# SSM layer: the next group's four x tiles ahead of z and their turn behind it, an output half and the later group's B and C after that, the decay exponents behind the third x

## The chip, the cores and the metric

The kernel runs on one core of one Trainium2 chip. The metric is device microseconds of one execution, as the median of several runs. TensorE (PE in the profile) multiplies matrices into PSUM, which has eight banks; VectorE (DVE) and ScalarE (ACT) read PSUM and work element by element; GpSimd (POOL) does elementwise work in SBUF alone; SyncE (SP) issues most transfers. Each engine takes its instructions in order and waits on semaphores for the others.

## The reference

One inference step of a two-layer hybrid model on 256 prompt tokens and 8 x 16 sample tokens, 384 tokens in all. Layer 0 has a short convolution and an attention, layer 1 is a state space mixer (SSM), and each layer ends in a feed-forward block with a convolution. The change touches only the SSM mixer:

```python
def odd_mixer(h, conv_state, ssm_state, w_in, conv_w, conv_b, dt_bias, a_log, d_skip, norm_w, w_out):
    proj = h @ w_in
    z, xbc, dt_raw = jnp.split(proj, [D_INNER, D_INNER + CONV_DIM], axis=-1)
    xbc, new_conv = causal_dwconv(xbc, conv_state, conv_w, conv_b)
    xbc = jax.nn.silu(xbc)
    xs, bm, cm = jnp.split(xbc, [D_INNER, D_INNER + SSM_GROUPS * D_STATE], axis=-1)
    dt = jax.nn.softplus(dt_raw.astype(f32) + dt_bias.astype(f32))
    a = -jnp.exp(a_log.astype(f32))
    y, h_last = ssd_scan(xs, dt, a, bm, cm, ssm_state, chunk)
    y = y + d_skip.astype(f32)[:, None] * xs.astype(f32)
    y = y.reshape(b, length, D_INNER) * jax.nn.silu(z.astype(f32))
    y = rms_norm(y.reshape(b, length, SSM_GROUPS, D_INNER // SSM_GROUPS), norm_w).reshape(b, length, D_INNER)
    return y.astype(h.dtype) @ w_out, new_conv, h_last
```

The scan forms, in each of four groups of eight heads, a product of C and B, weights it with decays exp(cum[q] - cum[s]) and dt, multiplies it with x, adds what comes from the state, and updates the state.

## The kernel before

All products are in float32 precision, made of three passes: a weight piece is split into a high part `wh` (ScalarE, L389 and L394) and a low part `wl` (VectorE, L390 and L395), the activations likewise into `Hh` and `Hl`, and `three` (L434) adds the products high-high, high-low and low-high. Weights come in one long stream of pieces of 128 x 1024, in the order in which `_pack` writes them (L83 to L151); `Weights.take` (L398) hands them out, and there are three buffers each for the raw piece, `wh` and `wl`. A piece is split as soon as TensorE is done with the piece three before it. Pieces of the output matrix are also scaled with the norm's gain; the table `gain` (L368) names them by their place in the stream.

The SSM layer goes through four groups (L1260). Per group it needs: one tile each of B and C and four tiles of x, every one a projection block of 24 matmuls (`conv4`, L951, in the profile `xbc`), then evacuated by VectorE into `pad` in two halves, scaled by ScalarE (`c`), three taps by VectorE (`c`), and a silu by ScalarE in two parts (`B`, `C`, `xf`). `turn_bc` (L993) makes the products of C and B (`cb`, masked into `CB` by VectorE) and turns B (`bT`); `turn_x` (L1018) turns the four x tiles in 12 transposes (`xT`), which ScalarE copies into `xt`. `decays` (L1031) loads the decay rows by four transfers (`td`), subtracts and clips on ScalarE, 16 instructions, and takes four exponents. `Group.__init__` multiplies `CB` into them, and into `mix` for the sample tokens, and makes the weighted copies of x, `xdt` on VectorE and `xw` on GpSimd. `skip` loads the eight old states (`h0`) and makes the skip terms. `within` is the part inside a group (`S`, `y`), `inter` what comes from the state (`yi`), `states` four state products `hn` at a time, which VectorE adds to `h0` before ScalarE's queue stores them. `project_z` is z, four pieces and 72 matmuls of 512 columns into three banks; `Gate` multiplies silu(z) in and makes the norm, `turn` turns the result (`yT`), and `add_out` is the group's share of the output product (`op`), four quarters of one piece, 24 matmuls each.

PSUM is split in the layer into three banks for the long products (`pmm`: `xbc`, `z`, `op`) and five for the others (`paux`), and each kind goes round. A product can begin only when the bank's last reader is done. The x tiles have four buffers, so the next group's tiles can be written once the last turn is over.

From L1218 to L1319 `T.keep` holds TensorE to the order in which the program is written. All other engines' orders are made by a scheduler. The order of a group before, for TensorE: `within`, `inter(2)`, one x tile (or 48 matmuls of `op`), `inter(1)`, `turn_bc`, another x tile, `states(0)`, z, `states(1)`, two x tiles, the later group's B, `turn_x`, its C, then the next group. Ahead of group 0 stand B, C and one x tile, then the sums of decays (`E`, `cT`, `sgS`, L1224 to L1248), which need dA, the end of a long chain of small VectorE instructions (`log1pexp`, L337).

Of the kernel before, what the change touches and what calls it, by code (L numbers as in the profile page):

```python
# [14 lines left out]
ALU = mybir.AluOpType  # L15
# [67 lines left out]
def _pack(x):  # L83
# [44 lines left out]
    def out(g, cs):  # L128
        for c in cs:
            for kt in range(4 * g, 4 * g + 4):  # L130
                blocks.append(wo[kt * P:(kt + 1) * P, c:c + 256])

    bc(0, 0), bc(1, 0), xs(0), bc(0, 1), bc(1, 1)
    for g in range(4):
        if 0 < g < 3:
            out(g - 1, (0, 256))
        if g < 3:
            xs(g + 1, (0, 1))
        if g == 1:
            out(0, (512, 768))  # L140
        tm(wi, 512 * g)
        if g < 3:
            xs(g + 1, (2, 3))
        if g < 2:
            bc(0, g + 2), bc(1, g + 2)
        if g == 2:
            out(1, (512, 768))
    out(2, (0, 256, 512, 768)), out(3, (0, 256, 512, 768))
# [95 lines left out]
def build(nc, tc, d, stop=None):  # L244
# [119 lines left out]
    class Weights:  # L364
        def __init__(self):
            self.tiles, self.made, self.raw, self.pos = {}, 0, None, 0

            t = 32 + 3 * NF + 8  # L368
            self.gain = {t + i: 4 * (0 if i < 16 else 1 if i < 36 else 2 if i < 44 else 3)
                         for i in (10, 11, 14, 15, 24, 25, 34, 35, *range(40, 48))}  # L370
            self.total = d["w"].shape[0] * (RC // WC)
# [675 lines left out]
    class Group:  # L1047

        def __init__(self, g, decs, bc, xt):
            self.g, self.h8, self.xt = g, slice(8 * g, 8 * g + 8), xt  # L1050
            self.Cg, self.Cm, self.CB, self.Bt, self.Bm = bc
            self.mix, self.xdt, self.xw, self.ys = [decs[0:2], decs[2:4]], [], [], []
            for b in range(2):
                for half in self.mix[b]:
                    tt(half, half, self.CB[:, b, :].unsqueeze(1).broadcast_to([P, 4, P]), ALU.mult)
            for b in range(3):
# [7 lines left out]
            mix = t512("mix", 1, (P, 8, P))  # L1064
            dsv = decS[:, 128 * g:128 * g + 128].rearrange("p (h j) -> p h j", j=LB)
            tt(mix.rearrange("p h (b j) -> p h b j", j=LB),
               tok_s(self.CB[:, 2, :]).unsqueeze(1).broadcast_to([P, 8, NB, LB]),
               dsv.unsqueeze(2).broadcast_to([P, 8, NB, LB]), ALU.mult)
            self.mix.append([mix[:, 0:4, :], mix[:, 4:8, :]])
# [68 lines left out]
    def project_z():  # L1138
        ps = yield from tm_group("z")
        zs = t512("zs", 1, (P, 3, 512))  # L1140
        for b in range(3):
            act(zs[:, b, :], ps[b], AF.Silu, scale=r[:, b:b + 1])
        return zs
# [76 lines left out]
    xs = [conv_x(0, 0)]  # L1220
# [30 lines left out]
    xs.append(conv_x(0, 1))  # L1251
    bc_ = turn_bc(0, Bn, Cn)
    xs += [conv_x(0, 2), conv_x(0, 3)]
    Bn = conv_bc(0, 1)
    xt = turn_x(xs)
    grp = Group(0, decs, bc_, xt)
    grp.skip()
    Cn = conv_bc(1, 1)
    op = gate = None
    for g in range(4):  # L1260
# [20 lines left out]
        if g == 1:  # L1281
            steps(op)
        zs = run(project_z())
        gate = Gate(grp.ys, False)
        for b in range(3):
            gate.part(b, zs)
        gate.factor()
        grp.states(1)
        xs += [conv_x(g + 1, 2), conv_x(g + 1, 3)]
        if g < 2:  # L1290
            Bn = conv_bc(0, g + 2)
        else:
            steps(op, 8)
        xt = turn_x(xs)
        grp = Group(g + 1, decs, bc_, xt)
        if g < 2:
            Cn = conv_bc(1, g + 2)
        else:
            steps(op)
# [43 lines left out]
```

## Time and profile before

| what | value |
|---|---|
| median of 3 runs (lowest to highest) | 1098.91 us (1098.24 to 1102.22) |
| the profiled execution | 1099.84 us, of which its span 1098.0 us |
| SSM layer, from its first projection to the next layer's first matmul | 459 to 816 us |
| in it: TensorE, VectorE, ScalarE, GpSimd busy | 315, 271, 186, 105 us of 357 |
| granted TensorE clock, mean of the span | 0.981 |

The busy times of the layer are the sums of its windows. A busy share is an average over stretches with different limits: VectorE with 271 of 357 is not the bound on the whole, but it may be where its instructions stand close. In the rows of the profile, `out<-in` names what an instruction writes and reads by the program's names, then come partitions x elements; in brackets stands the idle time of the engine just before it and what ended it. All VectorE products come from one helper line (L313), all ScalarE ones from L319, all matmuls from L253, so that they are told apart by their tiles.

### The profile page before, as it was taken

What the parts mean: (1) busy time and instruction counts of PE and PEld (TensorE: products, weight loads), DVE (VectorE), ACT (ScalarE), POOL (GpSimd) and SP (SyncE); (2) the same over time, 40 slices, a digit from 0 to 9 for tenths busy, and PEclk for the clock granted to TensorE, in tenths of its full rate; (3) what the DMA queues carried; (4) which work ended last, traced back from release to release, by engine and by line L of the source; (5) the groups of instructions that cost most, each with busy time, mean ns of one, the idle gap of its engine ahead of it and who ended that gap; (6) DMA issues with size and microseconds to landing.
All of it is one profiled execution on the core that took longest, in us unless ns stands there. A gap on an engine that the chain in (4) does not pass through costs nothing.

```text
span 1098.0 us, 16780 instructions
## 1 busy us (share of the span) xinstructions
PE 1045.0 (95%) x6316; PEld 972.7 (89%) x6316; DVE 740.5 (67%) x1329; ACT 491.9 (45%) x815; POOL 151.0 (14%) x383
## 2 busy tenths in 40 slices
PE   9999999999999999967997997998999999999998
PEld 6788899999999999957686885876899999999998
DVE  6968666767767544457777958768897776775332
ACT  6344334544444333347656445552564444443221
POOL 0030000100000000013606205416001000000000
PEclk9999999999999999978998998998999999999999
DMA  8452534343434434344273553462543444344441
GB/s 270 155 167 65 167 119 133 123 130 121 134 120 131 136 122 135 115 134 128 88 267 107 156 177 129 147 197 71 173 135 122 123 127 134 120 132 131 148 149 42
DMA packets 50329, 150.31 MB, mean 137 GB/s; under 512 B 5992, under 2 KB 8312, under 8 KB 50248
## 3 DMA queue, kind: packets, MB, share of 16 engines
q1 hardware_dynamic: 44360, 136.78, 40.1%
q10 hardware_dynamic: 4608, 8.39, 2.0%
q0 software_dynamic: 1280, 4.06, 1.0%
q8 instruction: 50, 0.82, 0.3%
q14 instruction: 31, 0.25, 0.1%
HBM read 135.81 MB, written 13.40 MB: 136 GB/s over the span
## 4 chain that ended last, share of the span: by engine, by line
PE 40%; DVE 9%; ACT 3%; DMA 3%; issue 2%; SPq 0%; DVEq 0%; ACTq 0%; POOL 0%
PE fd L253 8%; PE fg L253 8%; PE fa L253 8%; PE z L253 6%; PE op L253 4%; DVE wl L313 2%; PE xbc L253 2%; DVE c L316 2%; ACT wh L319 1%; DVE wl L316 1%; PE xT L258 1%; DMA raw<-w 1%; DVE pad L313 1%; PE y L253 1%; PE hn L253 1%
## 5 line engine op out<-in xcount | busy, mean ns | idle before, releaser
L313 DVE TENSOR_TENSOR wl<-raw,wh 128x1024 fp32r<-128x1024 f32 (+1 forms) x205 | 261.1, 1274 | 152.9 <-ACT wh L319 152.5
L319 ACT ACTIVATE wh<-raw 128x1024 fp32r<-128x1024 f32 (+1 forms) x205 | 216.1, 1055 | 249.3 <-PE fd L253 95.0
L253 PE MATMUL fg<-Hh,wh 128*128 128x384 f32 x352 | 118.4, 336 | 1.0 <-DVE pad L313 1.0
L253 PE MATMUL fa<-Hl,wh 128*128 128x384 f32 x352 | 118.7, 337 | 0.3 <-DVE Hl L316 0.3
L253 PE MATMUL fg<-Hl,wh 128*128 128x384 f32 x352 | 118.6, 337 | 0.0
L253 PE MATMUL fa<-Hh,wl 128*128 128x384 f32 x352 | 118.4, 336 | 0.0
L253 PE MATMUL fg<-Hh,wl 128*128 128x384 f32 x352 | 118.4, 336 | 0.0
L253 PE MATMUL fa<-Hh,wh 128*128 128x384 f32 x352 | 118.3, 336 | 0.0
L253 PE MATMUL fd<-hh,wh 128*128 128x384 f32 x352 | 118.3, 336 | 0.0
L253 PE MATMUL fd<-hh,wl 128*128 128x384 f32 x352 | 118.3, 336 | 0.0
L253 PE MATMUL fd<-hl,wh 128*128 128x384 f32 x352 | 118.3, 336 | 0.0
L316 DVE SCALAR_TENSOR_TENSOR c<-pad,prm,c 128x400 f32<-128x400 f32 (+1 forms) x160 | 103.0, 647 | 11.7 <-ACT c L319 9.8
L253 PE MATMUL xbc<-Hh,wh 128*128 128x384 f32 x192 | 68.9, 359 | 0.7 <-DVE X L313 0.7
L253 PEld LDWEIGHTS fg<-Hh,wh 128*128 128x128 f32 x352 | 66.2, 188 | 1.3 <-ACT R L319 1.3
L253 PEld LDWEIGHTS fa<-Hl,wh 128*128 128x128 f32 x352 | 66.2, 188 | 0.8 <-DVE Hl L316 0.6
L253 PEld LDWEIGHTS fa<-Hh,wl 128*128 128x128 f32 x352 | 66.2, 188 | 0.1
L253 PEld LDWEIGHTS fg<-Hh,wl 128*128 128x128 f32 x352 | 66.2, 188 | 0.1
L253 PEld LDWEIGHTS fg<-Hl,wh 128*128 128x128 f32 x352 | 66.2, 188 | 0.1
L253 PEld LDWEIGHTS fa<-Hh,wh 128*128 128x128 f32 x352 | 66.2, 188 | 0.1
L253 PE MATMUL xbc<-Hl,wh 128*128 128x384 f32 x192 | 66.2, 345 | 0.0
L253 PE MATMUL xbc<-Hh,wl 128*128 128x384 f32 x192 | 66.2, 345 | 0.0
L253 PEld LDWEIGHTS fd<-hl,wh 128*128 128x128 f32 x352 | 66.2, 188 | 0.0
(803 smaller groups left out, 2134.1 us busy)
## 6 DMA issues: line engine op xcount, KB each, us to landing
raw<-w SPq DMA_DIRECT2D x219, 512.0 KB, 3.5
kc<-kc SPq DMA_DIRECT2D x8, 256.0 KB, 4.8
vc<-vc SPq DMA_DIRECT2D x8, 256.0 KB, 3.2
X<-x SPq DMA_DIRECT2D x8, 192.0 KB, 4.4
o_y<-X SPq DMA_DIRECT2D x8, 192.0 KB, 2.7
o_v<-vt POOLq DMA_DIRECT2D x3, 256.0 KB, 2.6
o_k<-kraw POOLq DMA_DIRECT2D x3, 256.0 KB, 3.3
cst<-cst SPq DMA_DIRECT2D x1, 617.0 KB, 6.0
```

The source lines that it names most:

```text
L253: ins = nc.tensor.matmul(*a, **kw)
L258: ins = nc.tensor.transpose(*a, **kw)
L313: (eng or V).tensor_tensor(out=out, in0=a, in1=b, op=op)
L316: V.scalar_tensor_tensor(out=out, in0=a, scalar=s, in1=b, op0=op0, op1=op1)
L319: S.activation(out, a, f, **kw)
```

## The change

The x tiles of the next group are now all projected ahead of z, and turned behind it. In group 0 three of them stand ahead of the decay sums, and the fourth, and both B and C of group 1, ahead of the turn; the four decay exponents thereby come behind the third x tile. Both calls of `states` stand ahead of z. The next group's decay products and `mix` (`Group.__init__`) stand ahead of z too; what needs the turned x is put into a new method `take`, behind it. After that come the output half (groups 1 and 2), the later group's B and C, and after group 0 one x tile of group 2. z takes two weight pieces of 512 at a time and runs both through the first two token blocks, then through the third. The weights are packed in the new order and the table of gains follows it. Nothing that is computed changes.

```diff
-    bc(0, 0), bc(1, 0), xs(0), bc(0, 1), bc(1, 1)
-    for g in range(4):
...
+    bc(0, 0), bc(1, 0), xs(0), bc(0, 1), bc(1, 1), xs(1), tm(wi, 0)
+    bc(0, 2), bc(1, 2), xs(2, (0,)), out(0, (0, 256)), xs(2, (1, 2, 3)), tm(wi, 512), out(0, (512, 768))
+    bc(0, 3), bc(1, 3), xs(3), tm(wi, 1024), out(1), tm(wi, 1536), out(2), out(3)
...
     def project_z():
-        ps = yield from tm_group("z")
+
+        ps = [pmm(f"z{b}") for b in range(3)]
+        for k0 in range(0, KT, 2):
+            ws = [W.take(512) for _ in range(2)]
+            for bs in ((0, 1), (2,)):
+                for i, (wh, wl) in enumerate(ws):
+                    for b in bs:
+                        o = slice(b * P, (b + 1) * P)
+                        three(ps[b], Hh[:, k0 + i, o], Hl[:, k0 + i, o], wh, wl, k0 + i == 0, k0 + i == KT - 1)
+                        yield
...
     Cn = conv_bc(1, 0)
-    xs = [conv_x(0, 0)]
+    xs = [conv_x(0, i) for i in range(3)]
...
     decs = decays(0)
-    xs.append(conv_x(0, 1))
-    bc_ = turn_bc(0, Bn, Cn)
-    xs += [conv_x(0, 2), conv_x(0, 3)]
-    Bn = conv_bc(0, 1)
-    xt = turn_x(xs)
-    grp = Group(0, decs, bc_, xt)
+    grp = Group(0, decs, turn_bc(0, Bn, Cn))
+    xs.append(conv_x(0, 3))
+    Bn, Cn = conv_bc(0, 1), conv_bc(1, 1)
+    grp.take(turn_x(xs))
     grp.skip()
-    Cn = conv_bc(1, 1)
+    xs = [conv_x(1, 0)]
...
         decs = decays(g + 1)
-        if g:
+        if g == 0:
+            xs.append(conv_x(1, 1))
+        elif g == 1:
             steps(op, 16)
         else:
-            xs = [conv_x(1, 0)]
+            xs = [conv_x(g + 1, 0)]
         grp.inter(1)
         bc_ = turn_bc(g + 1, Bn, Cn)
-        xs = [conv_x(g + 1, 0)] if g else [*xs, conv_x(g + 1, 1)]
+        xs.append(conv_x(g + 1, len(xs)))
         grp.states(0)
-        if g:
-            xs.append(conv_x(g + 1, 1))
-        if g == 1:
-            steps(op)
+        while len(xs) < 4:
+            xs.append(conv_x(g + 1, len(xs)))
+        grp.states(1)
+        nxt = Group(g + 1, decs, bc_)
         zs = run(project_z())
         gate = Gate(grp.ys, False)
         for b in range(3):
             gate.part(b, zs)
+        xt = turn_x(xs)
         gate.factor()
-        grp.states(1)
-        xs += [conv_x(g + 1, 2), conv_x(g + 1, 3)]
...
+        grp = nxt
+        grp.take(xt)
+        if g:
+            steps(op)
         if g < 2:
-            Cn = conv_bc(1, g + 2)
-        else:
-            steps(op)
+            Bn, Cn = conv_bc(0, g + 2), conv_bc(1, g + 2)
+        if g == 0:
+            xs = [conv_x(2, 0)]
         grp.skip()
```

TensorE's order at z of group 0, before: one state product of four, then z, whose three banks are z_5335 to z_5337, from the first matmul on.

```order
L253 MATMUL hn<-xw__5027,Bm__4851 128x512 x4
L253 MATMUL z_5335<-wh,Hh 128x512
L253 MATMUL z_5335<-wl,Hh 128x512
L253 MATMUL z_5335<-wh,Hl 128x512
L253 MATMUL z_5336<-wh,Hh 128x512
L253 MATMUL z_5336<-wl,Hh 128x512
L253 MATMUL z_5336<-wh,Hl 128x512
L253 MATMUL z_5337<-wh,Hh 128x512
```

The same place of the change, behind its second hn (one more block of 24 `xbc` matmuls stands between the first hn and this one), up to the point where the third bank, z_5455, is first written:

```order
L240 MATMUL z_5453<-wh,Hl 128x512
L240 MATMUL z_5454<-wh,Hh 128x512
L240 MATMUL z_5454<-wl,Hh 128x512
L240 MATMUL z_5454<-wh,Hl 128x512
L240 MATMUL z_5453<-wh,Hh 128x512
L240 MATMUL z_5453<-wl,Hh 128x512
L240 MATMUL z_5453<-wh,Hl 128x512
L240 MATMUL z_5454<-wh,Hh 128x512
L240 MATMUL z_5454<-wl,Hh 128x512
L240 MATMUL z_5454<-wh,Hl 128x512
L240 MATMUL z_5455<-wh,Hh 128x512
```

The first two rows of z, left out above, follow the second hn directly. The third bank is first written twelve matmuls behind the start of z instead of six, and both state products stand ahead of it.

VectorE's order at the same place, before: `h__...` are the states, to which the products hn are added, `c_5308` the taps of the last x tile ahead of z, `mix` the sample tokens' decay products of group 1, and `wl` behind them weight splits of z.

```order
L313 TENSOR_TENSOR h__5031<-h__5031,hn 128x512
L313 TENSOR_TENSOR h__5035<-h__5035,hn 128x512
L316 SCALAR_TENSOR_TENSOR c_5308<-pad_5301,prm,c_5308 128x408
L313 TENSOR_TENSOR h__5039<-h__5039,hn 128x512
L316 SCALAR_TENSOR_TENSOR c_5308<-pad_5301,prm,c_5308 128x408
L313 TENSOR_TENSOR h__5043<-h__5043,hn 128x512
L316 SCALAR_TENSOR_TENSOR c_5308<-pad_5301,prm,c_5308 128x408
L313 TENSOR_TENSOR td__5191<-td__5191,CB__5255 128x512
L313 TENSOR_TENSOR mix__5670<-CB__5255,decS 128x1024
L313 TENSOR_TENSOR wl<-raw,wh 128x1024 x3
```

And in the change, from the second of these additions on; `pad_5413` is the evacuation of the fourth x tile, whose bank is z's third:

```order
L300 TENSOR_TENSOR h__5081<-h__5081,hn 128x512
L303 SCALAR_TENSOR_TENSOR c_5354<-pad_5347,prm,c_5354 128x408
L300 TENSOR_TENSOR h__5085<-h__5085,hn 128x512
L303 SCALAR_TENSOR_TENSOR c_5354<-pad_5347,prm,c_5354 128x408
L300 TENSOR_TENSOR h__5089<-h__5089,hn 128x512
L303 SCALAR_TENSOR_TENSOR c_5354<-pad_5347,prm,c_5354 128x408
L300 TENSOR_TENSOR td__5237<-td__5237,CB__5301 128x512
L300 TENSOR_TENSOR mix__5451<-CB__5301,decS 128x1024
L300 TENSOR_TENSOR pad_5413<-xbc,R 128x256
L300 TENSOR_TENSOR wl<-raw,wh 128x1024
L300 TENSOR_TENSOR pad_5413<-xbc,R 128x8x16
L300 TENSOR_TENSOR h__5079<-h__5079,hn 128x512
```

The order up to `mix` is the same; behind it stands the new tile's evacuation in two halves around a weight split, and then the second set of additions.

ScalarE's order ahead of the turn of group 0 (`xt`), before: the last x tile is `xf__4902`, made of `c_4941`, and the table load for its silu stands ahead of the second tile's, `xf__4792`, two tiles earlier.

```order
L319 ACTIVATE xf__4856<-c_4895 128x256
L319 ACTIVATE xf__4856<-c_4895 128x128
L319 ACTIVATE c_4941<-pad_4934,prm 128x408
L319 ACTIVATE c_4987<-pad_4980,prm 128x408
L319 ACTIVATE xf__4902<-c_4941 128x256
L319 ACTIVATE xf__4902<-c_4941 128x128
```

And in the change, where only the fourth tile, `xf__4908`, stands behind the exponents of `td`:

```order
L306 ACTIVATE td__4874<-td__4874 128x512
L306 ACTIVATE Bm__4897<-bT,cst 128x128 x2
L306 ACTIVATE c_4947<-pad_4940,prm 128x408
L306 ACTIVATE c_4993<-pad_4986,prm 128x408
L306 ACTIVATE wh<-raw 128x1024
L306 ACT_TABLE_LOAD
L306 ACTIVATE xf__4908<-c_4947 128x256
L306 ACTIVATE xf__4908<-c_4947 128x128
```

Three of the four tiles' silus now stand ahead of the exponents, where only the first stood before; the two that moved stand between two table loads more than before. The fourth has stayed behind the exponents, behind a weight copy and a table load.

More of the change, by code (lines that the diff above doesn't have):

```diff
@@ L126, in xs, with out @@
         fm(wi, [2048 + 512 * g + P * i for i in tiles])
-    def out(g, cs):
+    def out(g, cs=(0, 256, 512, 768)):
         for c in cs:
@@ L131, in out @@
                 blocks.append(wo[kt * P:(kt + 1) * P, c:c + 256])
-    bc(0, 0), bc(1, 0), xs(0), bc(0, 1), bc(1, 1)
-    for g in range(4):
[L135 to L138, printed above, removed]
-        if g == 1:
[L140 to L148, printed above, removed]
+    bc(0, 0), bc(1, 0), xs(0), bc(0, 1), bc(1, 1), xs(1), tm(wi, 0)
+    bc(0, 2), bc(1, 2), xs(2, (0,)), out(0, (0, 256)), xs(2, (1, 2, 3)), tm(wi, 512), out(0, (512, 768))
+    bc(0, 3), bc(1, 3), xs(3), tm(wi, 1024), out(1), tm(wi, 1536), out(2), out(3)
     ffn(1)
@@ L366, in __init__ @@
             self.tiles, self.made, self.raw, self.pos = {}, 0, None, 0
-            t = 32 + 3 * NF + 8
-            self.gain = {t + i: 4 * (0 if i < 16 else 1 if i < 36 else 2 if i < 44 else 3)
-                         for i in (10, 11, 14, 15, 24, 25, 34, 35, *range(40, 48))}
+            t, self.gain = 32 + 3 * NF + 8, {}
+            for g, at in enumerate(((11, 12, 20, 21), range(32, 36), range(40, 44), range(44, 48))):
+                self.gain.update({t + i: 4 * g for i in at})
             self.total = d["w"].shape[0] * (RC // WC)
@@ L1047, in build, with __init__ @@
     class Group:
-        def __init__(self, g, decs, bc, xt):
-            self.g, self.h8, self.xt = g, slice(8 * g, 8 * g + 8), xt
+        def __init__(self, g, decs, bc):
+            self.g, self.h8 = g, slice(8 * g, 8 * g + 8)
             self.Cg, self.Cm, self.CB, self.Bt, self.Bm = bc
@@ L1055, in __init__, with take @@
                     tt(half, half, self.CB[:, b, :].unsqueeze(1).broadcast_to([P, 4, P]), ALU.mult)
+            mix = t512("mix", 1, (P, 8, P))
+            dsv = decS[:, 128 * g:128 * g + 128].rearrange("p (h j) -> p h j", j=LB)
+            tt(mix.rearrange("p h (b j) -> p h b j", j=LB),
+               tok_s(self.CB[:, 2, :]).unsqueeze(1).broadcast_to([P, 8, NB, LB]),
+               dsv.unsqueeze(2).broadcast_to([P, 8, NB, LB]), ALU.mult)
+            self.mix.append([mix[:, 0:4, :], mix[:, 4:8, :]])
+        def take(self, xt):
+            self.xt = xt
             for b in range(3):
@@ L1063, in __init__ @@
                 self.xw.append(xw)
[L1064 to L1069, printed above, removed]
         def col(self, t, b, off=0):
@@ L1286, in build @@
             gate.part(b, zs)
+        xt = turn_x(xs)
         gate.factor()
-        grp.states(1)
-        xs += [conv_x(g + 1, 2), conv_x(g + 1, 3)]
+        grp = nxt
+        grp.take(xt)
+        if g:
+            steps(op)
         if g < 2:
-            Bn = conv_bc(0, g + 2)
-        else:
[L1293 to L1296, printed above, removed]
-            Cn = conv_bc(1, g + 2)
-        else:
-            steps(op)
+            Bn, Cn = conv_bc(0, g + 2), conv_bc(1, g + 2)
+        if g == 0:
+            xs = [conv_x(2, 0)]
         grp.skip()
```

1 line of the change is left out of this document (removed).

## The prediction

> **What bounds the kernel now.** I read the page from the top: span, busy shares, the 40 slices.
>
> ```profile
> span 1098.0 us, 16780 instructions
> PE 1045.0 (95%) x6316; PEld 972.7 (89%) x6316; DVE 740.5 (67%) x1329; ACT 491.9 (45%) x815; POOL 151.0 (14%) x383
> PE   9999999999999999967997997998999999999998
> PEclk9999999999999999978998998998999999999999
> ```
>
> TensorE is the bound nearly everywhere. Its row falls below 9 only between slice 17 and slice 28, which is the SSM layer (about 459 to 816 us), and the granted clock falls in the same slices. So the change, which touches only that layer, can win there what TensorE stands idle, plus what it then works at the lower clock. Next I read the timeline of TensorE there; the bracket is the idle time before a row and what ended it.
>
> ```profile
> 511.60 0.33 PE L258 MATMUL xT<-cst,xf__4856 128*128 128x128 f32 x1 [1.83 <-ACT xf__4856 L319]
> 516.26 0.48 PE L258 MATMUL xT<-cst,xf__4902 128*128 128x128 f32 x1 [4.33 <-ACT xf__4902 L319]
> ...
> 577.01 0.33 PE L258 MATMUL xT<-cst,xf__5497 128*128 128x128 f32 x1 [1.33 <-ACT xf__5497 L319]
> 582.32 0.48 PE L258 MATMUL xT<-cst,xf__5543 128*128 128x128 f32 x1 [4.99 <-ACT xf__5543 L319]
> ...
> 662.64 0.33 PE L258 MATMUL xT<-cst,xf__6319 128*128 128x128 f32 x1 [1.34 <-ACT xf__6319 L319]
> 667.96 0.48 PE L258 MATMUL xT<-cst,xf__6365 128*128 128x128 f32 x1 [4.98 <-ACT xf__6365 L319]
> ...
> 740.05 0.33 PE L258 MATMUL xT<-cst,xf__7060 128*128 128x128 f32 x1 [1.55 <-ACT xf__7060 L319]
> 744.75 0.48 PE L258 MATMUL xT<-cst,xf__7106 128*128 128x128 f32 x1 [4.38 <-ACT xf__7106 L319]
> ```
>
> Each of the four turns of x stands some 6 us, because the silus of the third and fourth tile are not done when the turn comes. The other waits are that of the decay sums, and one in each z:
>
> ```profile
> 484.40 3.25 PE L253 MATMUL E<-dA,cst 128*128 128x32 f32 x14 [8.16 <-DVE dA L316]
> ...
> 546.06 0.47 PE L253 MATMUL z<-wh,Hh 128*128 128x512 f32 x1 [1.47 <-DVE pad L313]
> ...
> 630.97 0.50 PE L253 MATMUL z<-wh,Hh 128*128 128x512 f32 x1 [1.61 <-DVE X L313]
> ...
> 708.81 0.47 PE L253 MATMUL z<-wh,Hh 128*128 128x512 f32 x1 [2.37 <-DVE pad L313]
> ```
>
> The windows say what the idle time costs behind it (the third number from the right is the granted clock):
>
> ```profile
> 478.40:492.10 13.70, 7.70 (x25) 5.57 (x26) 7.68 (x20) 3.98 (x8) 1.28 (x6) 0.50 0.37 121
> 512.60:519.40 6.80, 3.14 (x13) 3.15 (x14) 5.54 (x9) 3.23 (x8) 3.05 (x7) 0.50 0.26 77
> 580.80:587.60 6.80, 5.28 (x20) 5.28 (x21) 6.31 (x9) 3.43 (x8) 4.90 (x8) 0.50 0.25 77
> 666.20:673.00 6.80, 5.04 (x19) 5.05 (x20) 6.40 (x9) 3.42 (x8) 4.66 (x8) 0.50 0.22 77
> 673.00:741.30 68.30, 62.41 (x414) 52.65 (x412) 49.76 (x87) 37.08 (x72) 23.25 (x34) 1.00 0.51 163
> 741.30:748.10 6.80, 3.35 (x14) 3.35 (x15) 4.66 (x7) 2.87 (x6) 2.15 (x2) 0.50 0.46 160
> ```
>
> Behind every long wait stands a stretch of 6.8 us (once two of them) at half clock. About 2.5 us of idleness was enough: the window from 512.6 follows the wait of 1.83 and the first 0.7 of the one of 4.33. The z wait of 2.37, inside 673 to 741, brought none.
>
> **What goes.** The sum is made against the profiled execution, 1099.84 us for its span of 1098.0.
>
> (a) The turns of groups 1 to 3 move behind z. Their four tiles are then finished one z earlier, and z covers the silus:
>
> ```profile
> 541.00:564.00 23.00, 17.32 (x72) 13.37 (x72) 2.05 (x3) 1.00 0.63 206
> 562.71 0.44 PE L253 MATMUL xbc<-Hh,wh 128*128 128x384 f32 x1
> 575.30 0.27 PE L258 MATMUL xT<-cst,xf__5201 128*128 128x128 f32 x1
> ```
>
> The first row is z alone, 17.3 us for 72 matmuls; the other two bound three projection blocks, 12.59 us or 4.2 each. The waits that go are 1.33 + 4.99 + 1.34 + 4.98 + 1.55 + 4.38 = 18.6 us. Without z as cover they would return whole. TensorE worked at half clock from the end of each wait to the end of its window: 582.3 to 587.6, 668.0 to 673.0, 744.8 to 748.1, 13.6 us, of which half, 6.8, goes too. The turn's own 12 transposes stay.
>
> (b) z now goes through two weight pieces with the first two token blocks and only then with the third. So the third bank is needed twelve matmuls later (12 x 0.24 = 2.9 us). The old waits, 1.47 + 1.61 + 2.37 = 5.5, go; what takes their place is counted below.
>
> (c) The decay sums get 48 more projection matmuls ahead of them, 8.4 us against the wait of 8.16, so TensorE comes to them at 484.6. But the order puts one more weight split (1.1, a row below) on VectorE ahead of dA, and behind dA pieces of the new x tiles, of which one tap is
>
> ```profile
> 482.06 0.63 DVE L316 SCALAR_TENSOR_TENSOR c<-pad,prm,c 128x408 f32<-128x408 f32 x1
> ```
>
> Hence a wait of 1.0 for dA (485.5); of 2.2 for the masked dA, which stands behind two evacuations, a split and two taps (3.7 behind dA, while the first products take some 1.5); and of 1.7 for the last product, behind two taps and the copy of its own predecessor. That is 4.9 for 8.16: 3.3 gained. Half clock cost 3.9 (484.4 to 492.1); I expect one window, 3.4. Together 3.8. Bounds: from 8 (no new wait) to 0.
>
> (d) The turn of group 0 also needs a silu that stands behind the exponents on ScalarE:
>
> ```profile
> 490.14 0.33 SPq L1241 DMA_DIRECT2D rows<-cumQ  x1
> 496.88 1.27 ACT L319 ACTIVATE td__4764<-td__4764,cumK 128x128 f32<-128x128 f32 x4
> 505.48 1.05 ACT L319 ACTIVATE wh<-raw 128x1024 fp32r<-128x1024 f32 x1
> 507.67 1.28 ACT L319 ACT_TABLE_LOAD   x1
> ```
>
> The decay rows are there 6.7 us after their store is issued, which comes about 1 us later than before, so at 497.9. From there ScalarE has four such sets (4.7), three weight copies (3.2), four exponents (2.1), some small ones (2.0), the table (1.3) and the silu (0.5): 13.8, so 511.7. TensorE leaves the small products of (c) and B's turn at about 494.2 and has three blocks, 12.6, before the turn: 506.8, or 510.2 with the half clock of (c). The wait is 1.5 to 4.9 instead of 6.16; I take 3.0, a gain of 3.2. The two more table loads, 1.28 each, lie in waits that are counted already.
>
> Gone in all: 18.6 + 6.8 + 5.5 + 3.8 + 3.2 = 37.9.
>
> **What comes.** The second state product (hn) of a group now stands ahead of z, one block behind the first in group 0. Products take five banks in turn, so the second set needs the banks of the first, which VectorE must have added up. VectorE's order there is that of before:
>
> ```profile
> 541.90 1.09 PE L253 MATMUL hn<-xw__5027,Bm__4851 32*128 32x512 f32 x2 [0.48 <-DVE CB__5255 L313]
> 542.92 0.49 PE L253 MATMUL z<-wh,Hh 128*128 128x512 f32 x1
> ...
> 536.71 4.51 DVE L313 TENSOR_TENSOR wl<-raw,wh 128x1024 fp32r<-128x1024 f32 x1 [0.79 <-ACT wh L319]
> 545.31 0.61 DVE L313 TENSOR_TENSOR pad<-xbc,R 128x256 f32<-128x256 f32 x2
> 546.44 1.22 DVE L313 TENSOR_TENSOR wl<-raw,wh 128x1024 fp32r<-128x1024 f32 x1
> 549.34 0.67 DVE L313 TENSOR_TENSOR h__5039<-h__5039,hn 128x512 f32<-128x512 f32 x1
> 552.24 1.21 DVE L313 TENSOR_TENSOR mix__5670<-CB__5255,decS 128x1024 f32<-128x1024 f32 x1
> ```
>
> On the old clock of this stretch, the first set ends at 542.9, the block between at 547.1, and the third addition at 550.0: **a new wait of 2.8**. z would start at 550.7 and ask for its third bank at 553.6; that bank's evacuation stands behind mix and around a weight split (553.4 + 0.3 + 1.2 + 0.2 = 555.1): another 1.6. Queued behind the waiting hn are z and all that follows on TensorE. Group 1 has an output half in between, so hn is free; z's third bank waits about 2.0 (1.2 to 2.7, by the same pieces). In group 2, on the same clock, the first hn waits 1.3 for CB, which stands behind a blocked weight split, and ends at 542.3; two blocks and the second hn follow, until 551.7. z's second bank is now the one behind mix: asked for at 552.4, free at 555.1, 2.7; the third, two taps, a split and two half evacuations later, 1.3 more. Two of these places bring, I expect, a half-clock window, less what it hides of a following wait: 1.5 each. Sum 2.8 + 1.6 + 2.0 + 5.3 + 3.0 = 14.7. Bounds: zero, if VectorE is ahead by some 5 us, to twice that.
>
> Why VectorE is late there is the first of its rows: a split of 1.22 took 4.51.
>
> ```profile
> 535.07 1.03 POOL L313 TENSOR_TENSOR h__5043<-h__5043,E 128x512 f32<-128x512 f32 x1
> 539.08 1.03 POOL L313 TENSOR_TENSOR h__5045<-h__5045,E 128x512 f32<-128x512 f32 x1
> ...
> 761.11 6.99 DVE L313 TENSOR_TENSOR y__7290<-y__7290,xt__7198 128x512 f32<-128x512 f32 x1
> ```
>
> GpSimd ran products of two inputs one behind the other until 540.1, and the split ended 1.1 us after the run. The changed order leaves that run in place.
> The Trainium skill, "SBUF — State Buffer", section "Who interferes with whom", says that a VectorE instruction with two SBUF inputs and a GpSimd one that reads SBUF block each other, and the section "SBUF: two separate sides" that whoever starts first holds the pair for the whole instruction. By that a split would wait for one product at most, 2.2 us instead of 4.51, and the sum would be about 5 lower; the trace agrees on the blocking, but shows it through four products.
> The page "TensorE: Matmul & The Clock Gate", section "Why this matters for your kernels", of the same Trainium skill warns of idle gaps over about 3 us. By that alone my 2.8 would not cost a half-clock window and the sum would be 3 lower; the row of 512.6, behind 2.5, speaks against relying on it.
>
> Net 37.9 - 14.7 = 23.2, so 1099.84 - 23.2 = 1076.6; the median of the runs is 0.9 under the profiled one, which makes **1076**.
>
> **Rivals.** *The covers hold*: VectorE's additions come in time, the 14.7 vanish: 1061. For it: in group 1 there is slack already. Against: in-order VectorE, with its rows unchanged up to there. *VectorE becomes the bound*: with the projections packed, the new waits and their half clocks nearly double (26): 1087. For it: in 673 to 741 VectorE is busy 49.8 of 68.3, and that time shrinks. *The block ends with one product* (the rule above, as a mechanism here): the split ends 2.3 earlier (4.51 - 1.22 - 1.03), and the waits of groups 0 and 2 shrink by that: 1071. Against it stands the 4.51. *Nothing is gained*, the wait of the turn moving to another one: 1099. It would need the fourth silu to be late by a whole z, 17 us. *Slower*: GpSimd's run catches a split that TensorE needs at once. TensorE has two pieces in hand, 8.4 us; less copy and split themselves (2.3), a block above 6.1 stalls it, and 6.99 is in the trace. At 7 plus a half window, 3.4, in each of three groups: 31 for 23, so 1107.
>
> **How the numbers follow.** Forecast 0.52, covers hold 0.18, VectorE bound 0.15, one product 0.05, nothing 0.05, slower 0.05. The range 1058 to 1088 takes in the first three and the rule's case and leaves out the last two and the edges, some 2 in 10. A measurement of this kernel tells about 0.5% (5.5 us) from no change: faster 0.90, same 0.05, slower 0.05.
>
> **What would show it.** In the profile after: no idle time before xT in groups 1 to 3; 1.5 to 5 us before the one of group 0; half clock in two to four windows instead of six; an idle hn of 2 to 4 us before z of group 0, and z waits for pad in all three. I am wrong if hn finds its banks, if the clock stays full (lower), or if weight splits become releasers of TensorE (higher).

## The result, and the profile after

The change is faster, by 1.5 to 1.8%, which is less than forecast:

| | median, us (lowest to highest) | ratio to the kernel before, 95% interval |
|---|---|---|
| before, on the same chip | 1100.54 (1098.24 to 1102.22) | |
| the change | 1083.05 (1080.51 to 1087.00) | 0.9846, 0.9807 to 0.9884 |
| the change, timed once more on another chip (before: 1103.27) | 1082.64 (1080.91 to 1084.31) | 0.9819, 0.9802 to 0.9835 |

So 17 to 21 us were gained where 23 were forecast; 1076 was the predicted time, 1058 to 1088 the range. The page of the change:

```profile
span 1085.1 us, 16777 instructions
...
PE   9999999999999999997898999999999999999998
...
PEclk9999999999999999998999999999999999999999
```

TensorE's row is below 9 in three slices of the middle instead of five, the clock's in one instead of five. The profiled execution took 1087.00 us. The windows of the whole SSM layer, of before (first row) and of the change (second), show busy times of TensorE, its weight loads, VectorE, ScalarE and GpSimd, and the granted clock:

```profile
459.10:816.00 356.90, 315.11 (x1970) 270.44 (x1971) 270.93 (x497) 186.29 (x378) 104.69 (x172) 0.94 0.45 146
```

```profile
459.30:799.70 340.40, 314.38 (x1971) 268.47 (x1972) 270.08 (x496) 187.68 (x381) 115.91 (x172) 0.96 0.47 153
```

The layer lost 16.5 us, and nearly all of it is idle time of TensorE: 356.9 - 315.1 = 41.8 before, 340.4 - 314.4 = 26.0 now, 15.8 less. The half-clock stretches of the change:

```profile
489.50:496.40 6.90, 5.19 (x15) 2.99 (x16) 3.35 (x8) 6.07 (x9) 0.43 (x4) 0.51 0.58 191
513.40:516.80 3.40, 2.71 (x12) 2.71 (x13) 2.30 (x6) 2.36 (x7) 1.41 (x6) 0.52 0.51 159
544.20:547.60 3.40, 3.40 (x13) 3.40 (x12) 3.40 (x7) 1.32 (x3) 1.93 (x3) 0.51 0.25 100
629.50:632.90 3.40, 3.40 (x9) 2.62 (x9) 2.50 (x5) 0.86 (x2) 0.25 (x2) 0.51 0.93 354
667.10:670.50 3.40, 3.40 (x34) 1.90 (x36) 3.40 (x6) 0.68 (x3) 0.68 (x5) 0.50 0.87 292
687.50:690.90 3.40, 3.40 (x13) 3.40 (x12) 3.40 (x7) 0.61 (x2) 1.51 (x3) 0.52 0.19 76
```

TensorE worked 21.5 us in them, against 24.5 in those of before (7.70 + 3.14 + 5.28 + 5.04 + 3.35): half of the difference, 1.5 us, is gained. The clock's low stretches have become shorter but not fewer. The timeline of TensorE shows what waits are left:

```profile
485.74 1.77 PE L240 MATMUL E<-dA,cst 128*128 128x32 f32 x14 [1.04 <-DVE dA L303]
489.38 1.01 PE L240 MATMUL E<-h__4829,cst 128*128 128x256 f32 x2 [1.87 <-DVE h__4829 L300]
493.09 2.08 PE L240 MATMUL sgS<-h__4851,cst 128*128 128x512 f32 x2 [1.71 <-DVE h__4851 L300]
514.09 0.48 PE L245 MATMUL xT<-cst,xf__4908 128*128 128x128 f32 x1 [4.42 <-ACT xf__4908 L306]
538.18 1.13 PE L240 MATMUL hn<-xw__5075,Bm__4897 32*128 32x512 f32 x6
542.80 1.09 PE L240 MATMUL hn<-xw__5075,Bm__4897 32*128 32x512 f32 x2 [3.49 <-DVE CB__5301 L300]
549.79 1.52 PE L240 MATMUL hn<-xw__5075,Bm__4897 32*128 32x512 f32 x8
555.39 0.47 PE L240 MATMUL z<-wh,Hh 128*128 128x512 f32 x1 [1.08 <-DVE pad L300]
...
586.66 0.66 PE L245 MATMUL yT<-cst,y__5097 128*128 128x128 f32 x4 [1.55 <-ACT y__5097 L306]
591.05 1.10 PE L240 MATMUL S<-xw__5620,Bt__5308 128*128 128x512 f32 x2 [1.80 <-ACT S__5815 L306]
593.12 0.69 PE L240 MATMUL y<-xdt__5618,td__5231 128*64 128x64 f32 x16 [0.97 <-DVE yl L300]
628.10 0.47 PE L240 MATMUL z<-wh,Hh 128*128 128x512 f32 x1 [2.70 <-DVE pad L300]
666.96 1.89 PE L240 MATMUL S<-xw__6367,Bt__6003 128*128 128x512 f32 x2 [1.75 <-DVE yl L300]
685.88 1.09 PE L240 MATMUL hn<-xw__6371,Bm__6005 32*128 32x512 f32 x2 [0.94 <-DVE CB__6739 L300]
702.90 0.47 PE L240 MATMUL z<-wh,Hh 128*128 128x512 f32 x1 [1.75 <-DVE pad L300]
```

No xT of groups 1 to 3 waits any more. What is new is the sixth row: the last two parts of the first hn of group 0 wait 3.49 us for CB, and the second hn, in the row behind it, runs through in 1.52, little more than the 1.14 of those in groups 1 and 3.

One thing in this profile is not the change's. In the same 120 us of the feed-forward block, which the change leaves alone, before had 695 matmuls, and the change 681 (first and second row); in a second profile of the change there were 694 (third row):

```profile
880.00:1000.00 120.00, 120.00 (x695) 120.00 (x694) 84.80 (x146) 55.01 (x73) 8.89 (x56) 1.00 0.41 128
```

```profile
860.00:980.00 120.00, 120.00 (x681) 120.00 (x681) 83.97 (x142) 53.35 (x71) 8.75 (x56) 1.00 0.40 123
```

```profile
860.00:980.00 120.00, 120.00 (x694) 120.00 (x693) 85.02 (x145) 54.09 (x73) 8.44 (x54) 1.00 0.41 126
```

That execution ran 2% slower over the block, some 3.5 us, at a full granted clock. Hence its 1087.00, the highest of the four. The experiments are therefore compared by the length of the layer, from its first projection to the next layer's first matmul, beside the times.

### The profile page after: what moved, and what is told of

Same layout as the page of the kernel before. It is cut to its first block, busy times and chain, and to the rows that moved or that the text cites. A ratio compares the mean times of both kernels' runs of the same rounds, so it can differ in the third digit from the quotient of the medians.

```text
span 1085.1 us, 16777 instructions
## 1 busy us (share of the span) xinstructions
PE 1048.3 (97%) x6316; PEld 974.8 (90%) x6316; DVE 739.6 (68%) x1329; ACT 493.6 (45%) x817; POOL 161.7 (15%) x383
## 4 chain that ended last, share of the span: by engine, by line
PE 37%; DVE 13%; ACT 3%; issue 2%; DMA 2%; SPq 0%; DVEq 0%; POOL 0%; ACTq 0%
PE fg L240 9%; PE fd L240 8%; PE fa L240 8%; PE z L240 5%; DVE wl L300 4%; PE op L240 3%; DVE c L303 2%; ACT wh L306 1%; PE xbc L240 1%; PE yi L240 1%; DVE wl L303 1%; DVE pad L300 1%; PE y L240 1%; DVE X L300 1%; DMA td__4856<-rows 1%
## 5 line engine op out<-in xcount | busy, mean ns | idle before, releaser
L240 PEld LDWEIGHTS fd<-hh,wl 128*128 128x128 f32 x352 | 66.2, 188 | 0.0
```

Of the source, the lines that this page charges most:

```text
L240: ins = nc.tensor.matmul(*a, **kw)
```

## The experiments

The lengths of the layer are 356.9 us before and 340.3 in the first profile of the change; each is read from one profiled execution. That execution lay 3.95 us above the median of its runs in the first profile of the change, 3.51 above in e9 and 2.73 above in e8, 1.75 below in e4 and 1.73 below in e5, and within 1.2 of it in the other experiments. So a layer can be off by some us, and where it and the ratio disagree, the ratio has more executions behind it.

| run | layer, us | median, us | ratio to before (interval) |
|---|---|---|---|
| e1 turn of x ahead of z | 360.1 | 1103.28 | 1.0007 (0.9995 to 1.0020) |
| e2 z one piece at a time | 345.7 | 1088.39 | 0.9883 (0.9856 to 0.9911) |
| e3 beginning as before | 344.7 | 1087.42 | 0.9870 (0.9851 to 0.9889) |
| e4 decay products on VectorE | 326.1 | 1072.06 | 0.9735 (0.9709 to 0.9761) |
| e5 the change again | 336.9 | 1082.64 | 0.9819 (0.9802 to 0.9835) |
| e6 products of C and B earlier | 334.8 | 1077.40 | 0.9774 (0.9748 to 0.9800) |
| e7 before, decay products on VectorE | 353.0 | 1096.21 | 0.9936 (0.9921 to 0.9951) |
| e8 as e4, one more x tile ahead of the turn of y | 333.3 | 1074.33 | 0.9739 (0.9721 to 0.9758) |
| e9 as e4, second hn behind z | 339.0 | 1082.47 | 0.9800 (0.9756 to 0.9845) |
| e10 as e4, sums on VectorE too | 325.1 | 1067.98 | 0.9680 (0.9642 to 0.9718) |
| e11 as e4, with e6's edit | 328.9 | 1076.54 | 0.9748 (0.9713 to 0.9783) |
| e12 half of the decay products on VectorE | 333.9 | 1077.31 | 0.9756 (0.9725 to 0.9787) |

e1 to e4 ran on one chip (before there: 1101.69), e5 to e8 on another (1103.27), e9 to e12 on a third (1104.32), so across these groups the ratios are compared.

### The change once more (e5)

> The change once more, unaltered. The matmuls of the feed-forward block behind the SSM layer, which the change doesn't touch, stood 176.7 ns apart in its first profile and 173.3 in all others, some 3.5 us in all. Theory (that belongs to the execution, not to the program): 173.3 here, a layer of 340.3 give or take 1 us, and a profiled span of about 1081.5 us. Rival (the program brings it, by where its code or buffers lie): 176.7 again and a span of about 1085.

The spacing of the feed-forward matmuls was 173.3 ns, the span 1078.9 us: it belonged to the execution. The layer came out 3.4 us shorter than in the first profile, more than I had allowed; so differences below some 3 us between two profiles of different kernels say little.

### Which parts gain (e1, e2, e3)

```diff
         nxt = Group(g + 1, decs, bc_)
+        xt = turn_x(xs)
         zs = run(project_z())
...
-        xt = turn_x(xs)
         gate.factor()
```

> The change with one thing undone: the turn of the next group's x tiles stands ahead of z again, directly behind the second state product, in groups 1 to 3. Theory (z covers the silus of the third and fourth tile): the waits before xT come back, larger than the 6.3, 6.3 and 5.9 us of before, since no projection block stands between the fourth tile and the turn any more: about 9 us each, 27 in all, with some 7 us of half clock behind them, less up to 5.5 for z's bank waits, which they hide. The layer goes from 340.3 us to 365 to 372, the time to 1107 to 1115 us. Rival (the silus would be ready in any case, and the gain came from the other parts): no wait of over 2 us before xT, time within 3 us of the change.

The waits of the timeline in e1, for groups 1, 2 and 3:

```profile
558.52 0.47 PE L245 MATMUL xT<-cst,xf__5381 128*128 128x128 f32 x1 [7.12 <-ACT xf__5381 L306]
...
634.71 0.47 PE L245 MATMUL xT<-cst,xf__6076 128*128 128x128 f32 x1 [5.03 <-ACT xf__6076 L306]
638.96 0.48 PE L245 MATMUL xT<-cst,xf__6122 128*128 128x128 f32 x1 [3.78 <-ACT xf__6122 L306]
...
714.23 0.47 PE L245 MATMUL xT<-cst,xf__6819 128*128 128x128 f32 x1 [6.10 <-ACT xf__6819 L306]
718.48 0.48 PE L245 MATMUL xT<-cst,xf__6865 128*128 128x128 f32 x1 [3.78 <-ACT xf__6865 L306]
```

They sum to 25.8, about the 27 expected, but the layer rose by 20 to 23 us, less than the 25 to 32 expected: while TensorE stands there, VectorE catches up, and z's bank waits and the wait before yT are gone. The whole gain of the change is thus undone by this one edit, and z is the cover. It does not follow that the other parts are worth nothing: the waits before xT are larger here than in the kernel before (25.8 against 18.6 in these groups).

```diff
-        ps = [pmm(f"z{b}") for b in range(3)]
-        for k0 in range(0, KT, 2):
...
+        ps = yield from tm_group("z")
```

> The change with z running through one weight piece and all three token blocks at a time, as before. Theory: the third bank is asked for 6 matmuls, 1.4 us, sooner, so z's three waits of 1.08, 2.70 and 1.75 us grow by about 1.4 each, and one of them may bring a half-clock window more: the layer 340.3 plus 4 to 6, the time 1087 to 1089 us. Rival 1 (the prediction's term as it was worded, 2.9 us each): plus 8.7 and more. Rival 2 (later waits, of yT and S, take it up): no change within 1 us.

```profile
627.79 0.47 PE L240 MATMUL z<-wh,Hh 128*128 128x512 f32 x1 [3.63 <-DVE pad L300]
...
702.23 0.48 PE L240 MATMUL z<-wh,Hh 128*128 128x512 f32 x1 [3.16 <-DVE pad L300]
```

The second and third z waited 3.63 and 3.16 instead of 2.70 and 1.75, the first 1.69 instead of 1.08. So the waits grew by 0.6 to 1.4 us each, 3.0 in all, at or below the theory's 1.4 and far from the 2.9 of the first rival. The layer grew by 5.4 against the first profile, as the theory said, but by 8.8 against e5, which is the rival's figure. The waits speak for the theory; the worth of the pairs is 5 to 9 us, no nearer than that.

```diff
-    xs = [conv_x(0, i) for i in range(3)]
+    xs = [conv_x(0, 0)]
...
-    grp = Group(0, decs, turn_bc(0, Bn, Cn))
-    xs.append(conv_x(0, 3))
-    Bn, Cn = conv_bc(0, 1), conv_bc(1, 1)
-    grp.take(turn_x(xs))
-    grp.skip()
+    xs.append(conv_x(0, 1))
+    bc_ = turn_bc(0, Bn, Cn)
+    xs += [conv_x(0, 2), conv_x(0, 3)]
+    Bn = conv_bc(0, 1)
+    xt = turn_x(xs)
+    grp = Group(0, decs, bc_)
+    grp.take(xt)
+    grp.skip()
+    Cn = conv_bc(1, 1)
     xs = [conv_x(1, 0)]
```

> The change with the beginning of group 0 as before: one x tile ahead of the decay sums, the second ahead of the turn of B, then the third and fourth and B of group 1, the turn, and C of group 1 behind it; the x tile of group 1 that the change has there follows. Theory: the waits of the decay sums (8.2 us) and before the first xT (6.2) come back, where the change has 4.6 and 4.4, with a longer half-clock stretch: the layer 340.3 plus 5 to 7, the time 1088 to 1090 us. Rival (the wait of hn behind GpSimd's run takes it up, since that run would not be moved by as much): plus 2 or less.

The wait for dA was 7.94 and that of the first turn 7.38 in three pieces; the layer grew by 4.4 against the first profile, just under the theory, and by 7.8 against e5, just over it. Part of what the beginning loses comes back where the rival had it: the wait of hn for CB was 1.12 instead of 3.49. The new beginning is worth 4 to 8 us.

### What ate the rest: GpSimd's run (e4, e6, e7, e12)

VectorE and GpSimd in the change, ahead of the first hn of group 0. First VectorE, then the first and the last row of a run of ten GpSimd products and sums, which has two short copies and no idle time in it:

```profile
535.83 6.30 DVE L300 TENSOR_TENSOR wl<-raw,wh 128x1024 fp32r<-128x1024 f32 x1 [2.01 <-ACT wh L306]
542.05 0.61 DVE L300 TENSOR_TENSOR CB__5301<-cb,cst 128x256 f32<-128x256 f32 x2
```

```profile
530.25 1.06 POOL L300 TENSOR_TENSOR h__5077<-h__5077,E 128x512 f32<-128x512 f32 x1
...
539.79 1.25 POOL L300 TENSOR_TENSOR y__5095<-y__5095,xt__5046 128x512 f32<-128x512 f32 x1
```

The split began inside the run and ended 1.1 us behind it, as before; but it took 6.30 us now, not 4.51, and CB, which stands behind it, made hn wait. In the kernel before, a copy stood behind the eighth decay product, the split got through beside it, and the last sum came only behind the split:

```profile
540.07 1.20 POOL L961 COPY osm<-pad 128x3 f32<-128x3 f32 x1
...
541.38 1.25 POOL L313 TENSOR_TENSOR y__5049<-y__5049,xt__4994 128x512 f32<-128x512 f32 x1
```

In the change the last sum belongs to the run. So of the 1.8 us by which the hold grew, one half comes from the split's earlier start (535.83 for 536.71) and the other from its later end (542.13 for 541.22). The experiment takes the eight decay products off GpSimd:

```diff
-                tt(heads(h0[:, :]), heads(h0[:, :]), bc64(E[:, o:o + 8]), ALU.mult, G)
+                tt(heads(h0[:, :]), heads(h0[:, :]), bc64(E[:, o:o + 8]), ALU.mult)
```

> The change with the eight products of the old states with their decays, per group, on VectorE instead of GpSimd. Theory (a weight split that begins inside GpSimd's run of products is held to its end, and CB behind it on VectorE, on which hn waits): the splits of 6.30, 4.07 and 5.84 us take 1.2, the waits of hn (3.49 and 0.94) go, with a half-clock window behind the first; VectorE has 4.9 us more to do in each group, which costs part of that in z's bank waits: the layer 340.3 minus 3 to 6, the time 1077 to 1080 us. Rival (VectorE's amount of work is what decides there, not the hold): the waits of hn stay or grow and the layer grows by 5 to 15 us.

The gain was 14.2 us of the layer against the first profile and 10.8 against e5, and 9 to 12 us of time by the ratios, two to three times the 3 to 6 that I expected. In e4, VectorE and TensorE at the same place:

```profile
536.87 1.22 DVE L300 TENSOR_TENSOR wl<-raw,wh 128x1024 fp32r<-128x1024 f32 x1
538.62 0.41 DVE L300 TENSOR_TENSOR CB__5301<-cb,cst 128x256 f32<-128x256 f32 x1
```

```profile
538.24 1.71 PE L240 MATMUL hn<-xw__5075,Bm__4897 32*128 32x512 f32 x8
...
544.24 3.95 PE L240 MATMUL hn<-xw__5075,Bm__4897 32*128 32x512 f32 x8
```

The split takes 1.22, CB is done in time, and no hn waits for it. The second hn's eight parts now take 3.95 us where those of groups 1 to 3 take 1.14: that is the wait of 2.8 that the prediction had put there, and the trace names VectorE's first three additions, `h__5077`, `h__5081` and `h__5085`, as what these parts waited for. z's waits shrink from 1.08, 2.70 and 1.75 to none, 0.71 and 1.07, and three half-clock stretches of six go. So VectorE's lateness behind the run had reached all these places, and I had counted it only at hn. The eight products themselves find room: ahead of the split VectorE had stood idle for 1.13, 0.24 and 2.01 us in the change, and in e4 it has no idle time there.

Is it the hold, or CB's place behind it? In e6 the products of C and B stand one block earlier:

```diff
+        bc_ = turn_bc(g + 1, Bn, Cn)
         if g == 0:
             xs.append(conv_x(1, 1))
...
         grp.inter(1)
-        bc_ = turn_bc(g + 1, Bn, Cn)
```

> The change with the products of C and B and the turn of B moved ahead of the projection block (or the 48 output matmuls) that stood before them, so that CB stands ahead of the blocked weight split on VectorE; GpSimd's run of products stays. Theory (the hold makes VectorE late with everything, CB is only the first thing that TensorE misses): the wait of hn for CB (3.49 and 0.94 us) goes, but about as much comes back at the second hn or in z's bank waits, so the layer is 340.3 minus 0 to 3 us, and the split still takes 5 to 7 us. Rival (the cost is CB's place in the order alone): the layer shrinks by 6 to 9 us, both waits and their half-clock windows.

VectorE, GpSimd's last product, and TensorE in e6:

```profile
528.82 8.50 DVE L300 TENSOR_TENSOR td__5219<-td__5219,CB__5251 128x512 f32<-128x512 f32 x1
```

```profile
535.73 1.03 POOL L300 TENSOR_TENSOR h__5091<-h__5091,E 128x512 f32<-128x512 f32 x1
```

```profile
547.70 3.82 PE L240 MATMUL hn<-xw__5075,Bm__4897 32*128 32x512 f32 x6 [4.60 <-DVE h__5077 L300]
```

CB was through by 528.8, and now the next VectorE product with two SBUF inputs was held, for 8.50 us instead of 0.68, through eight GpSimd instructions to 537.3. The wait of hn for CB is gone and 4.60 at the second hn has come instead, so the mechanism is the theory's. Its size isn't: the layer lost 5.5 us against the first profile and 2.1 against e5, where 0 to 3 were expected, and by time e6 is 5.2 us faster than e5, on the same chip and with intervals that do not meet. With the run in place the earlier place of CB is thus worth some 5 us, a little less than the 6 to 9 of the rival.

> The kernel before with the eight decay products per group on VectorE instead of GpSimd. Theory (the hold costs much only where the second hn and z's late bank press upon VectorE, that is in the change): the layer of before, 356.9 us, shrinks by 2 to 6, mainly by z's bank waits of 5.5 us, to a time of 1094 to 1098 us, so that without the hold the change is worth 25 to 29 us instead of 17. Rival (the hold cost before as much as it does behind the change): the layer shrinks by 11 to 14 us and the time to 1086 to 1089.

The same edit in the kernel before gained 3.9 us of layer, and 0.64% of time, 7 us, against 9 to 12 in the change: less pressed upon the hold there, but it cost something already. Without the run the change is worth 0.9735 / 0.9936 = 0.980, 22 us of 1100 (two chips, so by ratios), below the 25 to 29 expected; by the layers, 353.0 against 326.1, it would be 27.

```diff
-                tt(heads(h0[:, :]), heads(h0[:, :]), bc64(E[:, o:o + 8]), ALU.mult, G)
+                tt(heads(h0[:, :]), heads(h0[:, :]), bc64(E[:, o:o + 8]), ALU.mult, G if par else None)
```

> The change with four of the eight decay products per group on VectorE, those of the first state product, and four on GpSimd. Theory (the length of GpSimd's run behind the start of the split decides): the run is 4 us shorter, so the first split of 6.30 us takes 2 to 3.5, the wait of hn for CB goes or is under 0.5, and the layer is 326 to 331. Rival (VectorE's amount of work is a burden of its own that was covered by the gain): with 2.4 us less of it per group than with all eight on VectorE, the layer is 324 or less. Second rival (the hold needs no run, any four products do as much): 336 or more.

The layer, 333.9, lies between the theory and the second rival. The splits were free, but the scheduler put a VectorE decay product into the rest of the run:

```profile
529.01 4.38 DVE L300 TENSOR_TENSOR h__5077<-h__5077,E 128x512 f32<-128x512 f32 x1
```

It takes 0.68 alone; in group 2 one took 5.62. A shorter run holds a different instruction; it is not a harmless one. By time, though, the ratio of 0.9756 is not told apart from e4's 0.9735, so most of the gain is had with four products moved.

### Repairs on top of e4 (e8 to e11)

```diff
-    bc(0, 2), bc(1, 2), xs(2, (0,)), out(0, (0, 256)), xs(2, (1, 2, 3)), tm(wi, 512), out(0, (512, 768))
+    bc(0, 2), bc(1, 2), xs(2, (0, 1)), out(0, (0, 256)), xs(2, (2, 3)), tm(wi, 512), out(0, (512, 768))
...
-            for g, at in enumerate(((11, 12, 20, 21), range(32, 36), range(40, 44), range(44, 48))):
+            for g, at in enumerate(((12, 13, 20, 21), range(32, 36), range(40, 44), range(44, 48))):
...
-            xs = [conv_x(2, 0)]
+            xs = [conv_x(2, 0), conv_x(2, 1)]
```

> The decay products on VectorE, as in the run before that had them there (layer 326.1 us), and in group 0 one more x tile of group 2 projected behind z (two instead of one, the weights packed accordingly), so that four blocks stand between the turn of x and that of the normalised y instead of three, and group 1 has one block fewer ahead of its z. Theory (the norm's chain on VectorE and ScalarE needs longer than three blocks cover): the wait before yT (1.1 us) and most of those behind it, of S and y (2.8), go, while z of group 1 loses cover and may wait 1 more: the layer 322 to 325. Rival (these waits are set by VectorE's amount of work, and move on): 326 or more.

The wait before yT did go, but S waited for ScalarE, whose copy stands behind more of the x and C tiles' work:

```profile
595.02 2.05 PE L240 MATMUL S<-xw__5620,Bt__5308 128*128 128x512 f32 x2 [6.86 <-ACT S__5861 L306]
```

The rival is right that the wait moved; its reason, VectorE's amount of work, isn't shown, since what S waited for is ScalarE. The layer is 7.2 us longer than in e4, but the ratio (0.9739 for 0.9735) shows neither gain nor loss.

```diff
         grp.states(0)
...
-        grp.states(1)
         nxt = Group(g + 1, decs, bc_)
...
         gate.factor()
+        grp.states(1)
```

> The decay products on VectorE (layer 326.1 us there), and the second state product behind z again, as in the kernel before. Theory (the prediction's wait of the second hn for the third addition, 2.8 us, is there once TensorE no longer waits earlier: its eight parts take 3.95 us instead of 1.07 with the products on VectorE, with a half-clock window in z behind it): that wait of 2.9 and about 1.7 of half clock go, while four additions, 2.4 us, come into the stretch of the norm's chain and lengthen the wait before yT by up to that: the layer 322 to 325. Rival (the second hn costs nothing, VectorE's lateness would only show at z's bank): 326 or more, with a wait of 3 us or more in z of group 0.

The theory fell: the layer is 12.8 us longer than in e4, in an execution above its median, and the ratio is 0.9800 for 0.9735, some 7 us, with intervals that just overlap. z's bank waits in groups 0 and 2:

```profile
550.43 0.47 PE L240 MATMUL z<-wh,Hh 128*128 128x512 f32 x1 [3.45 <-DVE pad L300]
...
695.36 0.77 PE L240 MATMUL z<-wh,Hh 128*128 128x512 f32 x1 [3.86 <-DVE pad L300]
```

Without the second hn ahead of it z starts sooner and waits for the evacuation of its third bank instead, and hn behind the turn then waits 0.5, 0.5 and 1.15 us for banks that the turn has used. The place of the second hn ahead of z costs nothing net; the wait there and z's are one lateness of VectorE, seen at two places.

```diff
-            tt(self.ys[b], self.ys[b], yi, ALU.add, None if late else G)
+            tt(self.ys[b], self.ys[b], yi, ALU.add)
```

> The decay products and the additions of what comes from the state to y on VectorE, so that GpSimd has no product or sum in that stretch at all. Theory (single GpSimd instructions hold VectorE for 1.1 us at most, and the two additions cost VectorE 0.67 each): the rows of 1.76 and 1.54 us go back to 0.7 and 0.6, the layer stays within 2 us of 326.1. Rival (any GpSimd sum there costs as the run did): 322 or less.

As the theory said, within 2 us in the layer (325.1). Its time, 1067.98 us, ratio 0.9680, is the best here, 3% under the kernel before; against e4's 0.9735 the intervals overlap, so that this last step is better is likely, not shown.

> The decay products on VectorE, and the products of C and B moved ahead of the block that stood before them. Theory (CB's place matters only while the run holds VectorE): hn has no wait for CB as it is, so the layer stays within 1.5 us of 326.1. Rival (CB's place has a worth of its own, as the layer of 334.8 against 336.9 to 340.3 with the run in place may mean): 323 or less.

The layer is 2.8 us longer than in e4, outside the 1.5 of the theory though within what two profiles of one kernel differ by, and its ratio is no lower than e4's: without the run CB's place has no gain of its own, against the rival.

## Why the prediction was right or wrong

The direction, the place and the bound were right: the gain is idle time of TensorE in the SSM layer. By sums, idle time was forecast to fall by 18.6 + 5.5 + 3.3 + 3.2 - 11.7 = 18.9 us and fell by 15.8; half clock was to give 6.8 + 0.5 - 3.0 = 4.3 and gave 1.5. These two errors, 3.1 and 2.8 us, are nearly all of the difference between the forecast of 23.2 and the layer's 16.5; the slow feed-forward block of the one profile comes on top of it. In e5 the layer was 20.0 us shorter than before, so about half of this difference is no more than what two profiles of the change differ by.

- (a) The turns behind z: right. All xT waits of groups 1 to 3 are gone (18.6 forecast), and e1 shows that z is what covers them.
- (b) z in pairs: right as a mechanism, worth 5 to 9 us (e2). The sentence "needed twelve matmuls later" was wrong: twelve behind z's start, but only six later than before, 1.4 us. The sum didn't use it.
- (c) The decay sums: 1.04 + 1.87 + 1.71 = 4.62 us of waits, where 1.0 + 2.2 + 1.7 = 4.9 were forecast; one half-clock window with 5.19 us of work in it, a loss of 2.6 where 3.4 was taken.
- (d) The turn of group 0: 4.42 instead of 3.0, near the upper bound of 4.9. ScalarE, its tables and the decay rows in the change:

```profile
491.91 0.33 SPq L1241 DMA_DIRECT2D rows<-cumQ  x1
...
499.94 1.28 ACT L306 ACTIVATE td__4856<-td__4856,cumK 128x128 f32<-128x128 f32 x4 [2.68 <-DMA td__4856<-rows]
...
511.43 1.28 ACT L306 ACT_TABLE_LOAD   x1
513.62 0.62 ACT L306 ACTIVATE xf__4908<-c 128x256 f32<-128x256 f32 x2 [0.91 <-DVE c L303]
```

  The store came at 491.9, 0.8 later than forecast, and the rows were used 8.0 us behind it instead of 6.7; the turn could begin at 514.1, where the silu had been forecast to end at 511.7.
- What comes: 11.7 forecast, and here a step failed. "VectorE's order there is that of before" held, but "on the old clock" did not, nor did "the changed order leaves that run in place" in time: GpSimd's run ended 1 us later (541.0 for 540.1), with the last sum now in it, though TensorE's S had come 2.3 earlier (520.6 for 523.0), so that the run held the split for 6.30 us. The wait therefore stood at the first hn, 3.49 instead of the old 0.48, and the second hn, forecast at 2.8, found its banks nearly free (1.52 for 1.14). That was the prediction's own sign of being wrong (though it was to make the time lower, not higher), and the "idle hn of 2 to 4 us" that it had named is there by luck, at another hn and for another reason. The mechanism named for the second hn is real: with the run gone it shows (3.95 for 1.14, e4), and with CB ahead of the run it is 4.60 (e6). z's banks and hn of group 2 came smaller: 1.08 for 1.6 in group 0, and 0.94 + 1.75 for 5.3 in group 2; group 1 had 2.70 for 2.0. That these places sum to 10.0 us, near the 11.7, is therefore in part luck.
- Not foreseen: the wait before yT of group 0 (1.55 and a smaller one of 0.41), longer ones of S and y behind it (1.80 and 0.97), and a longer one of S in group 2 (1.75 for 1.05), together some 4.5 us more than before. The turn of x now stands between z and the norm's chain, and brings its copies and products on ScalarE, VectorE and GpSimd there. The traces show that chain longer: from `v` to `rg` VectorE needed 2.8 us before (566.34 to 569.13) and 7.2 in the change (575.84 to 583.02), of which 2.5 is in three small operations beside GpSimd's products (the row at the end of this document is one) and 1.66 in four weight splits between them. That taking these away would end the wait is argued: no run did, e8 only moved it.
- Half clock: two new windows were forecast and four stood outside the beginning, each of 3.4 us, in which TensorE worked throughout: 4 x 1.7 = 6.8, where 3.0 was taken. The sign "two to four windows instead of six" failed with it; there are six.
- Rivals: *the block ends with one product* is refuted, by 6.30 us and by e6's 8.50. By that the rule in the Trainium skill, "SBUF — State Buffer", section "SBUF: two separate sides", that the pair of SBUF ports which the two engines share is held for the whole instruction, understates it here: the split was kept out from one GpSimd product to the next. When it gets in is not settled: before, it got through beside a copy behind the products, which took 1.20 us, and in the change two copies of 0.18 and 0.20 us and one more sum went ahead of it. *VectorE becomes the bound* was nearest among the rivals (1087, 4 us off where the forecast is 7 off), but its reason was not the one: e4 gives VectorE more work (749.4 us busy in its page, 739.6 in that of the change) and is faster by about 1%. *Covers hold*, *nothing gained* and *slower* did not come about.

## What to carry to other kernels

Sort the waits of an in-order engine by who is late, not by where TensorE stands: hn, z's bank and again hn were one lateness of VectorE, and each repair at a place moved it (e6 gave some 5 us of time, and e8 and e9 gave nothing on top of e4), while the repair at its cause (e4) gave 9 to 12. Cheap elementwise products in one unbroken GpSimd run are dear where VectorE has two-input work due in that time. The plain sum doesn't tell it: eight products cost VectorE 8 x 0.68 = 5.4 us, and the run had added 6.30 - 1.22 = 5.1 to the split. What counts is where the time falls: on VectorE the products filled idle time ahead of the split, on GpSimd they delayed what TensorE waits for. And when a change shifts engines against each other, work out the overlap anew for each; a row that keeps its place in the order doesn't keep its place in time.

## What the runs showed of the hardware

A half-clock stretch came behind little idle time in one place: in the change the hn of group 2 waited 0.94 us, between products of 32 rows, and the clock halved 1.6 us behind it (687.5); the prediction had counted on some 2.5 us. The stretches lasted 3.4 or 6.8 us in the change, where those of before lasted 6.8 or two such. The small VectorE operations of the norm's chain, 0.16 us alone, took up to 1.0 us beside GpSimd's products, as one of them shows, first before, where GpSimd stood idle, then in the change, where it ran products from 573.8 to 579.4:

```profile
567.20 0.17 DVE L326 TENSOR_SCALAR rqm<-rqi 128x3 int32<-128x3 int32 x1
...
578.37 1.00 DVE L313 TENSOR_SCALAR rqm<-rqi 128x3 int32<-128x3 int32 x1
```

And the feed-forward block ran at 176.7 ns for each matmul in some profiled executions (the first of the change, e9, e11) and at 173.3 in the others, also of the same kernel, at the same granted clock; why stays open.
